# A hybrid attention layer on one core: low weight parts moved to the left end of the buffer, deeper rings for split parts and raw rows, and the order of the last steps' splits

## Chip, cores, metric

One core of a Trainium2 chip. The kernel's time is device microseconds (us) from start to end of one execution; lower is better. A measurement tells two kernels apart when they differ by about 0.5% or more.

## The reference, cut to what matters

One layer over 1024 tokens of width 1024, batch 1, float32:

```python
h = rms_norm(x, mix_norm_g)
u = h @ w_in          # dq, dk, dv | bq, bk, bv | z : 512 columns each, z 1024
dq, dk = rms_norm per 64 columns;  bq, bk = rms_norm per 64 columns
a = diff_attention(dq, dk, dv)     # 4 heads, two softmaxes each, subtracted, ALiBi; then rms_norm
b = dilated_attention(bq, bk, bv)  # 8 heads, windows (128,1) (512,4) (2048,16), merged, ALiBi
y = concat([a, b]) * silu(z)
x = x + y @ w_out
x = x + sigmoid(rms_norm(x, ple_norm_g) @ w_ple_gate) * (p @ w_ple_proj)
```

## The kernel before

Every float32 operand of a large product is split into a high and a low part (hi by a ScalarE copy that rounds, lo = source - hi on VectorE or GpSimd), and a product is three matmuls: hi*hi, hi*lo, lo*hi. The program runs in four stages.

**Stage 1** (0 to 158 us) projects bq, bk and bv from h. It writes bv, bq and bk split to memory outside the core. **Stage 2** (158 to 384 us) runs the eight heads of the dilated attention; the projections of dq, dk and dv are its filler. A step handles one unit (head, kind, u): scores of the unit two ahead (`scores`, L593), their minimum (`least`, L613, VectorE) and exponentials (`exps`, L622, ScalarE), four transposes of this unit (`turn`, L633 and L640 to L645) into one of two PSUM buffers with the tag `t` (pool `ps_t`), the high part by ScalarE (L646), the low part by VectorE (L651, this frees the buffer), and the value products of the unit two back (`values`, L681, L693). Between these `filler(n)` puts n matmuls of the projection (L503, L505, L507). A finished row block of dq or dk (columns c, token tile t) goes by `rows_out` into a `raw` buffer (L426, ScalarE), is squared on GpSimd and summed on VectorE. After four tiles (a group g) a chain of small steps computes factors and scales the four raw blocks (L462, three on GpSimd, one on VectorE). Then the generator `turned(g, ...)` transposes the group in four pieces (L483) into the same two `t` buffers; `cut` splits each piece into `hi` (ScalarE, L469) and `lo` (VectorE, L470, this frees the `t` buffer), and stores both by DMA (L472). `turn_part` advances it by one yield and is called twice in a step: after `turn_lo` and after `values`. The generator first lets TURN_WAIT calls pass. The value blocks of dv go through `v_out` (L417, L418, stores L419) and take their buffers from the same rings, tags `qkhi` and `qklo`.

**Stage 3** (384 to 661 us) runs the differential attention in 36 steps, with the z projection and the first two blocks of the output projection as filler (`z_part(n)`, n matmuls, called a tick each; `pending` holds calls that are due after so many ticks). `weights_at(m, at)` splits weight block m: high part on ScalarE (L895) after `at` ticks, low part on GpSimd (L900) four ticks later. `values(k, 1)` leaves a closure in `slot` that reads the finished PSUM buffer (squares, L1167, on ScalarE; a product into `asb`, L1169, on VectorE); `in_slot` runs it at the start of the next step. The one buffer of that pool also takes `pss` (L1185). `y_split` (L1247, L1248) splits a finished y block. **Stage 4** is the rest of the output projection and the gate.

**Order.** In stage 2 the order on TensorE and GpSimd is the order of the program text; ScalarE, VectorE and the SP queue (nearly all DMAs) are put in order by a planner. In stage 3 all five are in program order, but for the first loads and z products, which the planner places; the loads `td`, `qs`, `kh`, `kl`, `vd` and the first `zraw` carry a raised priority.

**Buffers.** A stage's pools are stacked from the left end or from the right end of each partition. A tile in a place that an earlier tile held waits for that tile's last reader. Bytes within a partition (from the built program):

```
left end                                   right end
stage 1  weights raw    74240 -  90624     (x, later squares 172544-, split rows bq/bk/bv 176640-186880)
         raw rows       90624 - 119296
         high, low     119296 - 172544
stage 2  w2r            74240 -  82432     kn 210944-220160  vn 220160-224768  qn -228864
         w2h            82432 -  98816     w2l 194560-210944   tb1 191488-194560
         free           98816 - 113152     raw2 177152-189440  sq2 -191488   tb2 175616-177152
                                           vc 159232-167424  e 167424-175616
                                           ph, oo 144896-159232  hi, lo 136704-144896
                                           pl, fold, extra 125440-136704  qc, kc 113152-125440
stage 3  zraw, zhi, zlo 74240 -  92672     kl_0 216576-224768  kh_0 208384-216576
         kh_1           92672 - 100864     qs 200192-208384    td 196096-200192
         rb            100864 - 104960     kl_1 187904-196096  ed 167424-187904
         zt, vd        104960 - 121344     phd, pld, sqd 141824-167424
```

Of the kernel before, what the change touches and what calls it, by code (L numbers as in the profile page):

```python
# [8 lines left out]
F32 = mybir.dt.float32  # L9
F32R = mybir.dt.float32r  # L10
# [8 lines left out]
P = 128  # L19
# [23 lines left out]
OUT_AT = 2  # L43
SUM_AT = 12
SPLIT_AT = 6
TURN_WAIT = 5
FOLD_AT = 1
CL_AT = {(1, 3): (0, 1), (0, 0): (2,)}
LAG = 2
# [22 lines left out]
def tile_hybrid_layer(ctx: ExitStack, tc, xT, w_att, w_z, w_o, w_g, w_p, pT, vec, lamv, tdil, tdiff, outT):  # L72
# [67 lines left out]
    def pool(name, bufs=1, **kw):  # L140
        return tc.tile_pool(name=name, bufs=bufs, reuse_waits="tile", **kw)
# [42 lines left out]
    with ExitStack() as pa:  # L184
# [77 lines left out]
        for d in range(8):  # L262
            g = vec_sb[:, C_G1 + d : C_G1 + d + 1]
            b, a = divmod(d, 2)
# [98 lines left out]
    with ExitStack() as pb:  # L363
        wpr = pb.enter_context(pool("w2r"))
        wph = pb.enter_context(pool("w2h"))
        np_ = pb.enter_context(pool("np", side="right"))
        wpl = pb.enter_context(pool("w2l", side="right"))
        tbp = pb.enter_context(pool("tbp", side="right"))
        ap_ = pb.enter_context(pool("ap2", side="right"))
        tbq = pb.enter_context(pool("tbq", side="right"))  # L370
        bpa = pb.enter_context(pool("bpa", side="right"))
        bpb = pb.enter_context(pool("bpb", side="right"))
        aq = pb.enter_context(pool("aq2", side="right"))
        bp = pb.enter_context(pool("bp", side="right"))
        cq = pb.enter_context(pool("cq", side="right"))
        ps_m = pb.enter_context(pool("ps_m", 2, space=PSUM))
        ps_t = pb.enter_context(pool("ps_t2", 2, space=PSUM))
        ps_s = pb.enter_context(pool("ps_s", 2, space=PSUM))
# [5 lines left out]
        turns, turns_done = [], []  # L384
# [11 lines left out]
        def proj():  # L396
# [15 lines left out]
            def v_out(t, ps):  # L412

                for a in range(2):
                    vt = aq.tile([P, 2, 2, P], F32R, tag="qkhi" if a else "qklo", bufs=2, name=f"v2_{t}_{a}")
                    v = ps[:, a * 256 : a * 256 + 256].rearrange("p (h w) -> p h w", w=P)
                    A.activation(vt[:, :, 0, :], v, AF.Copy, scale=rstd[:, t : t + 1])  # L417
                    V.scalar_tensor_tensor(out=vt[:, :, 1, :], in0=v, scalar=rstd[:, t : t + 1], in1=vt[:, :, 0, :].bitcast(F32), op0=ALU.mult, op1=ALU.subtract)  # L418
                    nc.sync.dma_start(dv_d[t * P : (t + 1) * P, 2 * a : 2 * a + 2].rearrange("t h w -> t (h w)"), vt.rearrange("p h a w -> p (h a w)").bitcast(F32))  # L419


            def rows_out(c, t, ps, ss, raws):
                g = 2 * c + t // 4
                assert 4 * g + t % 4 < 6 or divmod(4 * g + t % 4 - 6, 4) in turns_done
                raw = ap_.tile([P, 512], F32, tag="raw", bufs=6, name=f"raw2_{c}_{t}")
                A.copy(raw, ps)  # L426
                sq = ap_.tile([P, 512], F32, tag="sq", bufs=1, name=f"sq2_{c}_{t}")
                G.tensor_mul(sq, raw, raw)
                raws.append((raw, sq))
# [34 lines left out]
            def cut(g, p_, fh, tp):  # L464
                n, t0 = ("dq", "dk")[g // 2], 512 * (g % 2) + 256 * p_
                gain = qk_scale(n)
                tv = tp.rearrange("p f a w -> p f (a w)")
                hi, lo = (aq.tile([P, 2, 256], F32R, tag=f"qk{k}", bufs=2, name=f"{k}2_{g}_{p_}_{fh}") for k in ("hi", "lo"))
                A.activation(hi, tv, AF.Copy, scale=gain)  # L469
                V.scalar_tensor_tensor(out=lo, in0=tv, scalar=gain, in1=hi.bitcast(F32), op0=ALU.mult, op1=ALU.subtract)  # L470
                for s_, tl in enumerate((hi, lo)):
                    nc.sync.dma_start(qk_d[n][2 * fh : 2 * fh + 2, :, s_, t0 : t0 + 256].rearrange("f p t -> p f t"), tl.bitcast(F32))  # L472
# [302 lines left out]
    with ExitStack() as pb:  # L775
# [106 lines left out]
        def zpath():  # L882
# [52 lines left out]
            def weights_at(m, at):  # L935
                pending.append([at, lambda: split_hi(m)])
                pending.append([at + 4, lambda: split_lo(m)])
# [52 lines left out]
            for f in range(2):  # L990
                for half in range(2):
                    held[f, half] = (ps_s[0] if f else ps_z).tile([P, 512], F32, tag="s" if f else "z", name=f"pso_{f}_{half}")
                if f == 0:
                    for h in range(2):
                        weights_at(18 + h, 3 + 23 * h)
                wo[f] = [ws[16 + 2 * f + b] for b in range(2)]
                for ds in (range(4), range(4, 6)):
                    for half in range(2):
                        for d in ds:
                            for _ in out_products(f, half, d):  # L1000
                                yield
# [242 lines left out]
        def y_split(i, half, src):  # L1244
            y_tile(i, half)
            hi, lo = y[half][i]
            A.copy(hi, src)  # L1247
            V.tensor_sub(lo, src, hi.bitcast(F32))  # L1248
# [33 lines left out]
        def in_slot():  # L1282
            for f in slot:
                f()
            slot.clear()

        def step(g):
# [36 lines left out]
            if g - 1 in Y_IN:  # L1324
                y_diff(*Y_IN[g - 1])
            if g in (32, 33):
                y_split(6, g - 32, ga[2, g - 32][0])
            if g == 33:
                bit(100)
# [271 lines left out]
```

## Time and profile before

| | us |
|---|---|
| median of 3 runs | 844.51 (844.06 to 846.97) |
| the profiled execution: its own time | 845.52 |
| its span in the trace | 843.6 |
| TensorE busy / granted clock over the span | 820.1 (97%) / 0.992 |
| VectorE, ScalarE, GpSimd busy | 541.6, 458.0, 335.2 |

Busy time is the sum of the instructions' durations where they don't overlap. The granted clock is the share of full speed that TensorE was given; it has two levels, 2.4 GHz (1.00) and 1.2 GHz (0.50), so a mean between them is a mixture. In a timeline row the brackets hold the engine's idle time just before the instruction and what ended it.

### The profile page before, as it was taken

Reading aid. Unit: us, or ns where it says so; the run is one execution under the profiler, and the core shown is the slowest. Engines: PE = TensorE matmul, PEld = TensorE weight load, DVE = VectorE, ACT = ScalarE, POOL = GpSimd, SP = SyncE. Lnnn points to the kernel's source line nnn. Section 1 sums busy time; section 2 is a strip of 40 time slices with the busy share of each in tenths; the row PEclk is TensorE's granted clock in tenths of the full one; section 3 lists DMA queues with packets and bytes.
Section 4 is the critical chain, followed back from the end, with each engine's and each line's share of the span. In section 5 each row is a group of like instructions: output and inputs, shape, how many; then the busy total and the mean of one; then the engine's idle time right before and its main releaser. Section 6 shows DMA issues by size and latency. Waiting matters only on the chain.

```text
span 843.6 us, 13212 instructions
## 1 busy us (share of the span) xinstructions
PE 820.1 (97%) x4364; PEld 696.3 (83%) x4364; DVE 541.6 (64%) x1264; ACT 458.0 (54%) x940; POOL 335.2 (40%) x391
## 2 busy tenths in 40 slices
PE   9999999999999999998999999999998999999997
PEld 8888888888878888887678878888787888888886
DVE  6948543467867686765688777778774573544432
ACT  8653433466766776664487876787671343321210
POOL 5503020145763555022278888785572243200000
PEclk9999999999999999999999999999999999999999
DMA  7612679558768679838597683944491574524210
GB/s 248 215 62 62 205 211 322 156 119 240 208 183 203 184 213 273 236 103 232 153 230 190 184 254 114 271 126 151 161 388 38 176 261 149 175 102 149 88 50 37
DMA packets 112468, 150.21 MB, mean 178 GB/s; under 512 B 11008, under 2 KB 70032, under 8 KB 112400
## 3 DMA queue, kind: packets, MB, share of 16 engines
q1 hardware_dynamic: 109376, 144.00, 56.7%
q10 hardware_dynamic: 3024, 5.38, 2.0%
q8 instruction: 34, 0.56, 0.3%
q14 instruction: 34, 0.28, 0.1%
HBM read 101.95 MB, written 47.39 MB: 177 GB/s over the span
## 4 chain that ended last, share of the span: by engine, by line
PE 80%; POOL 5%; DMA 4%; DVE 4%; ACT 3%; issue 2%; SPq 1%; DVEq 0%; POOLq 0%; ACTq 0%
PE mm L253 5%; PE mm L255 5%; PE mm L254 5%; PE mm L503 5%; PE mm L507 5%; PE mm L505 5%; PE psg L1401 3%; PE psg L1402 3%; PE psg L1403 3%; PE s L593 3%; PE pso L1403 3%; PE pso L1401 3%; PE pso L1402 3%; POOL ed L1122 2%; PE sd L1098 2%; PE sd L1099 2%
## 5 line engine op out<-in xcount | busy, mean ns | idle before, releaser
L1122 POOL TENSOR_TENSOR ed<-ed,ed 128x512 f32<-128x512 f32 x64 | 82.1, 1304 | 51.1 <-ACT ed L1120 34.1
L1110 ACT ACTIVATE ed<-ed,nm 128x1024 f32<-128x1024 f32 x64 | 73.8, 1153 | 45.9 <-DVE nm L1101 45.9
L622 ACT ACTIVATE e<-e,stats 128x256 f32<-128x256 f32 x128 | 64.7, 508 | 30.8 <-DVE stats L613 30.5
L503 PE MATMUL mm<-w2h,h_hi 128*128 128x512 f32 x192 | 79.0, 412 | 0.7 <-ACT raw L426 0.7
L505 PE MATMUL mm<-w2l,h_hi 128*128 128x512 f32 x192 | 79.5, 414 | 0.0
L507 PE MATMUL mm<-w2h,h_lo 128*128 128x512 f32 x192 | 76.7, 400 | 0.0
L254 PE MATMUL mm<-wl,h_hi 128*128 128x512 f32 x192 | 75.3, 392 | 0.0
L255 PE MATMUL mm<-wh,h_lo 128*128 128x512 f32 x192 | 75.1, 391 | 0.0
L253 PE MATMUL mm<-wh,h_hi 128*128 128x512 f32 x192 | 74.5, 394 | 0.0
L613 DVE CUSTOM_DVE_ANT_0 e<-s,tb 128x256 f32<-128x256 f32 x128 | 48.8, 418 | 18.6 <-PE s L593 18.0
L651 DVE TENSOR_TENSOR pl<-t,ph 128x512 fp32r<-128x512 f32 (+2 forms) x72 | 45.1, 627 | 19.9 <-ACT ph L646 17.7
L1101 DVE CUSTOM_DVE_ANT_0 ed<-sd,td,nm 128x512 f32<-128x512 f32 x64 | 48.1, 751 | 12.3 <-PE sd L1099 3.3
L1098 PE MATMUL sd<-kh,qs 128*128 128x512 f32 x128 | 54.2, 423 | 0.8 <-DVE nm L1101 0.4
L1101 DVE CUSTOM_DVE_ANT_0 ed<-sd,td 128x512 f32<-128x512 f32 x64 | 43.9, 686 | 14.8 <-PE sd L1099 11.7
L943 PE MATMUL psz<-h_hi,zhi 128*128 128x512 f32 x128 | 50.7, 396 | 1.1 <-ACT zhi L895 1.1
L947 PE MATMUL psz<-h_hi,zlo 128*128 128x512 f32 x128 | 50.8, 397 | 0.6 <-POOL zlo L900 0.6
L1099 PE MATMUL sd<-kl,qs 128*128 128x512 f32 x128 | 50.7, 396 | 0.7 <-DMA kl<-dk_d 0.7
L945 PE MATMUL psz<-h_lo,zhi 128*128 128x512 f32 x128 | 50.7, 396 | 0.0
L646 ACT CAST ph<-t 128x512 fp32r<-128x512 f32 (+2 forms) x72 | 38.2, 532 | 22.9 <-PE t L633 13.4
L1143 DVE TENSOR_TENSOR pld<-td,phd 128x512 fp32r<-128x512 f32 x64 | 42.2, 687 | 12.8 <-ACT phd L1134 12.3
L1401 PE MATMUL psg<-h,wh_g 128*128 128x512 f32 x128 | 50.0, 391 | 0.0
L1403 PE MATMUL psg<-h,wl_g 128*128 128x512 f32 x128 | 49.8, 389 | 0.0
(283 smaller groups left out, 2325.5 us busy)
## 6 DMA issues: line engine op xcount, KB each, us to landing
kn<-bk_d SPq DMA_DIRECT2D x16, 512.0 KB, 7.1
w2r<-in_w_att_dram SPq DMA_DIRECT2D x24, 256.0 KB, 4.3
y<-yd_d SPq DMA_DIRECT2D x12, 512.0 KB, 6.8
x<-in_xT_dram SPq DMA_DIRECT2D x16, 256.0 KB, 5.4
wr<-in_w_att_dram SPq DMA_DIRECT2D x8, 512.0 KB, 3.8
qn<-bq_d SPq DMA_DIRECT2D x16, 256.0 KB, 4.1
bv_d<-bv SPq DMA_DIRECT2D x16, 256.0 KB, 4.4
vc<-bv_d SPq DMA_DIRECT2D x32, 128.0 KB, 4.6
```

Of the source, the lines that this page charges most:

```text
L253: T.matmul(ps, h_hi[d][:, ts_], wh, start=(d == 0), stop=False)
L254: T.matmul(ps, h_hi[d][:, ts_], wl, start=False, stop=False)
L255: T.matmul(ps, h_lo[d][:, ts_], wh, start=False, stop=(d == 7))
L503: T.matmul(ps, h_hi[d][:, ts_], wh, start=(d == 0), stop=False)
L505: T.matmul(ps, h_hi[d][:, ts_], wl, start=False, stop=False)
L507: T.matmul(ps, h_lo[d][:, ts_], wh, start=False, stop=(d == 7))
L1098: T.matmul(ps, q, kh[:, c, hs], start=True, stop=False)
L1101: V.tensor_tensor_reduce(out=sp[:, hs], in0=ps, in1=td[:, off : off + 512], scale=4.0 ** -(hd + 1), scalar=BIG if half == 0 else nm[:, 0:1 ...
L1110: A.activation(sp, sp, AF.Exp, bias=nm[:, 1:2], scale=-1.0, accum_out=l)
L1122: G.tensor_add(w[:, hs], w[:, hs], e1[:, hs])
L1401: T.matmul(ps, hi[:, d, :], xh, start=(d == first), stop=False)
L1403: T.matmul(ps, lo[:, d, :], xh, start=False, stop=(d == last))
```

## The change

In stage 2 the pool of the low weight parts (`w2l`) goes from the right end to the left end, behind `w2h`, where stage 1 had its raw rows. The rings of `qkhi` and `qklo` get four buffers each for two, the ring `raw` eight for six, and TURN_WAIT is 8 for 5. The pools `cq` (qc, kc) and `aq2` (hi, lo) change places with `bpb` (ph, oo) and `bp`. In stage 3 the second half of weight block 19 is split after 33 ticks for 26, and in steps 32 and 33 `in_slot` is called ahead of `y_split`.

```diff
-TURN_WAIT = 5
+TURN_WAIT = 8
@@ stage 2, pools
         wpr = pb.enter_context(pool("w2r"))
         wph = pb.enter_context(pool("w2h"))
+        wpl = pb.enter_context(pool("w2l"))
         np_ = pb.enter_context(pool("np", side="right"))
-        wpl = pb.enter_context(pool("w2l", side="right"))
         tbp = pb.enter_context(pool("tbp", side="right"))
         ap_ = pb.enter_context(pool("ap2", side="right"))
         tbq = pb.enter_context(pool("tbq", side="right"))
         bpa = pb.enter_context(pool("bpa", side="right"))
+        cq = pb.enter_context(pool("cq", side="right"))
+        aq = pb.enter_context(pool("aq2", side="right"))
         bpb = pb.enter_context(pool("bpb", side="right"))
-        aq = pb.enter_context(pool("aq2", side="right"))
         bp = pb.enter_context(pool("bp", side="right"))
-        cq = pb.enter_context(pool("cq", side="right"))
@@ v_out
-                    vt = aq.tile([P, 2, 2, P], F32R, tag="qkhi" if a else "qklo", bufs=2, name=f"v2_{t}_{a}")
+                    vt = aq.tile([P, 2, 2, P], F32R, tag="qkhi" if a else "qklo", bufs=4, name=f"v2_{t}_{a}")
@@ rows_out
-                assert 4 * g + t % 4 < 6 or divmod(4 * g + t % 4 - 6, 4) in turns_done
-                raw = ap_.tile([P, 512], F32, tag="raw", bufs=6, name=f"raw2_{c}_{t}")
+                assert 4 * g + t % 4 < 8 or divmod(4 * g + t % 4 - 8, 4) in turns_done
+                raw = ap_.tile([P, 512], F32, tag="raw", bufs=8, name=f"raw2_{c}_{t}")
@@ cut
-                hi, lo = (aq.tile([P, 2, 256], F32R, tag=f"qk{k}", bufs=2, name=f"{k}2_{g}_{p_}_{fh}") for k in ("hi", "lo"))
+                hi, lo = (aq.tile([P, 2, 256], F32R, tag=f"qk{k}", bufs=4, name=f"{k}2_{g}_{p_}_{fh}") for k in ("hi", "lo"))
@@ zpath, first block of the output projection
-                        weights_at(18 + h, 3 + 23 * h)
+                        weights_at(18 + h, 3 + 30 * h)
@@ step of stage 3
             if g in (32, 33):
+                in_slot()
                 y_split(6, g - 32, ga[2, g - 32][0])
```

## Rows read from the trace of the kernel before

**Rows 1.** The page's first part: busy time, share of the span and instructions of each engine.

```profile
PE 820.1 (97%) x4364; PEld 696.3 (83%) x4364; DVE 541.6 (64%) x1264; ACT 458.0 (54%) x940; POOL 335.2 (40%) x391
```

**Rows 2.** TensorE's waits over the whole span: what waited for what; us in total, how often, the longest.

```profile
PE pss L1185 <- DVE asb L1169: 2.1, 1, 2.1
PE tp L483 <- POOL raw L462: 2.0, 2, 1.5
PE tp L483 <- DVE lo L470: 1.6, 1, 1.6
PE t L633 <- DVE lo L470: 1.2, 1, 1.2
...
PE psz L943 <- ACT zhi L895: 1.1, 1, 1.1
...
PE sd L1099 <- DMA kl<-dk_d: 0.7, 1, 0.7
PE mm L503 <- ACT raw L426: 0.7, 1, 0.7
PE psz L947 <- POOL zlo L900: 0.6, 1, 0.6
```

**Rows 3.** Busy time by stretch: the stretch and its length, then busy us (instructions) of TensorE, weight loads, VectorE, ScalarE and GpSimd, then TensorE's granted clock, the DMA engines' share and GB/s.

```profile
210.00:220.00 10.00, 10.00 (x64) 8.68 (x63) 9.54 (x22) 7.81 (x19) 7.11 (x8) 1.00 0.72 211
...
235.00:240.00 5.00, 2.98 (x16) 2.23 (x15) 3.94 (x11) 2.80 (x8) 4.92 (x5) 0.97 0.86 281
240.00:245.00 5.00, 5.00 (x27) 4.45 (x25) 2.79 (x7) 2.49 (x7) 3.48 (x4) 0.69 0.55 158
...
320.00:330.00 10.00, 8.43 (x56) 7.33 (x55) 6.75 (x17) 6.09 (x17) 4.97 (x9) 1.00 1.00 275
...
410.00:415.00 5.00, 5.00 (x17) 3.92 (x16) 3.15 (x7) 3.06 (x7) 2.69 (x3) 0.66 0.29 105
...
600.00:605.00 5.00, 4.38 (x18) 3.75 (x18) 3.46 (x11) 3.60 (x6) 2.41 (x3) 0.66 0.74 254
...
640.00:645.00 5.00, 2.71 (x13) 2.63 (x14) 2.74 (x6) 0.00 (x0) 0.96 (x1) 0.74 0.00 0
```

**Rows 4.** Timeline of TensorE around two of group 0's transposes and one of group 1's, and of GpSimd's scaling of group 1: start, duration, engine, line, operation, count.

```profile
201.87 0.60 PE L483 MATMUL tp<-ident,raw 128*128 128x128 f32 x4
205.32 0.60 PE L483 MATMUL tp<-ident,raw 128*128 128x128 f32 x4
...
238.67 0.55 PE L483 MATMUL tp<-ident,raw 128*128 128x128 f32 x3 [1.54 <-POOL raw L462]
...
235.20 4.42 POOL L462 TENSOR_TENSOR raw<-raw,fac_dq 128x512 f32<-128x512 f32 x3
```

**Rows 5.** Timeline of VectorE, SP and ScalarE around the two late cuts, and, from the view of one line, the time from issue to landing of the four stores of line 419 between 310 and 332 us.

```profile
296.58 0.75 DVE L470 SCALAR_TENSOR_TENSOR lo<-tp,vec_sb,hi 128x512 fp32r<-128x512 f32 x1 [2.43 <-DMA dk_d<-lo]
...
318.49 0.54 SPq L419 DMA_DIRECT2D dv_d<-v  x1
...
327.03 0.69 ACT L469 ACTIVATE hi<-tp,vec_sb 128x512 fp32r<-128x512 f32 x1 [2.37 <-PE o L693]
...
DMA to landing us min/median/max: 5.0/5.7/8.4
```

**Rows 6.** Timeline of TensorE, SP and VectorE at the change from stage 2 to stage 3, and the load of `rb` with its time to landing.

```profile
383.88 0.28 PE L693 MATMUL o<-pl,vn 128*128 128x256 f32 x1
...
383.72 0.33 SPq L790 DMA_DIRECT2D td<-in_tdiff_dram  x1
386.82 2.98 SPq L810 DMA_DIRECT2D kl<-dk_d  x4
402.60 1.06 SPq L890 DMA_DIRECT2D zraw<-in_w_z_dram  x2
...
138.44 0.43 SPq L1338 DMA_DIRECT2D rb<-rs_d  x1
DMA to landing us min/median/max: 7.4/7.4/7.4
...
395.28 0.70 DVE L952 TENSOR_TENSOR psz<-psz,rb 128x512 f32<-128x512 f32 x1 [4.66 <-PE psz L947]
```

**Rows 7.** Timeline of VectorE, ScalarE and GpSimd in the last steps of stage 3.

```profile
638.35 0.16 DVE L110 TENSOR_TENSOR dtmp<-dfac 128x4 f32<-128x4 f32 x1
638.55 1.21 DVE L112 SCALAR_TENSOR_TENSOR dtmp<-dtmp,sub 128x4 f32<-128x4 f32 x1
640.90 0.68 DVE L1248 TENSOR_TENSOR y<-ya,y 128x512 fp32r<-128x512 f32 x1
641.58 0.41 DVE L1169 TENSOR_TENSOR asb<-od,zt 128x256 f32<-128x256 f32 x1
...
637.75 0.62 ACT L895 CAST zhi<-zraw 128x512 fp32r<-128x512 f32 x1 [1.71 <-PE pso L1013]
...
638.45 1.29 POOL L900 TENSOR_TENSOR zlo<-zraw,zhi 128x512 fp32r<-128x512 f32 x1 [2.20 <-ACT zhi L895]
```

**Rows 8.** Timeline of ScalarE and GpSimd where stage 2 takes over from stage 1.

```profile
159.02 1.07 ACT L426 COPY raw<-mm 128x512 f32<-128x512 f32 x2 [4.48 <-DVE stats L613]
...
109.45 2.01 POOL L571 CAST qc<-qn 128x1024 fp32r<-128x1024 f32 x1
159.69 1.04 POOL L428 TENSOR_TENSOR sq<-raw 128x512 f32<-128x512 f32 x1 [47.92 <-ACT raw L426]
```

## The prediction

> **What bounds the kernel now.** I read the page first: TensorE is busy 820.1 of 843.6 us [rows 1], the next engine 541.6. So nothing but TensorE's own time sets the end, and an edit can win only what TensorE loses: idle time, and time at the lower clock. The second view is therefore the list of TensorE's waits [rows 2]. The reader is to see that the waits are few, each with its own cause, and that eight of them lie at places that the diff touches: 2.1 + 2.0 + 1.6 + 1.2 + 1.1 + 0.7 + 0.7 + 0.6 = 10.0 us. The third view, busy time by stretch [rows 3], shows what a wait costs behind it. After the idle time in 235 to 240 the granted clock is 0.69 in the next 5 us: between the levels of 1.00 and 0.50 that is (1 - 0.69) x 5 = 1.55 us of lost work, and 0.15 in the stretch before, together 1.7. In 410 to 415 it is 0.34 x 5 = 1.7, in 640 to 645 0.26 x 5 = 1.3. Not every wait brings it: after the 1.6 us in 320 to 330 the clock is 1.00, yet it fell to 0.66 in 600 to 605, where TensorE idled for only 0.6. I take the clock's loss where the rows show it, and give no rule for it. The fourth view is the timeline at each wait, for its cause.
>
> **The change part by part.** Which tile lies over which follows from the sizes in the table of buffers. After the change, from the left: w2l 98816-115200. From the right: tb1 207872-210944, raw and sq 189440-207872, tb2 -189440, vc 171520-179712, e -187904, kc and qc 159232-171520, hi and lo 142848-159232, oo and ph 128512-142848, then pl, fold, extra from 117248.
>
> *First raw copies.* raw2 lies over stage 1's split rows of bv, and its first copy waits until 159.02 [rows 8], though ScalarE was idle for 4.48 us. The last stores of bv are what it waits for, in my reading of the addresses. Afterwards it lies over tiles of x, long free. TensorE's wait of 0.7 for it [rows 2] goes: **-0.7**. In exchange e comes over the split rows; e is first written at about the time of that copy, so I put it at nothing (at worst the same 0.7 comes back). The copy into qc, 2.01 us, has to wait for stage 1's last weights, because qc now lies over them; GpSimd stands idle for 47.92 us up to 159.69 [rows 8], which hides it. w2l over the raw rows costs nothing: w2h, which is written first, lay over raw rows that are freed no earlier.
>
> *TURN_WAIT 8.* Three more calls at two in a step are 1.5 steps. Two transposes of a group, one step apart, start at 201.87 and 205.32 [rows 4], so a step is 3.45 us and a group's transposes move 5.2 us later. In group 1 the scaling on GpSimd ends at 235.20 + 4.42 = 239.62, and the transposes wait for it, the last of them until 238.67 [rows 4], 2.0 us in all [rows 2]; 5.2 us later nothing is left of that. With the clock behind it: 2.0 + 1.7 = **-3.7**. The eight raw buffers are what lets the transposes come later; they cost nothing by themselves.
>
> *Four buffers for hi and lo.* At 296.58 a cut on VectorE waits 2.43 us for the store of an older `lo` [rows 5], and a transpose of the attention behind it waits 1.2 for the `t` buffer [rows 2]. At 327.03 ScalarE's `hi` has idled 2.37 us; the row names TensorE, but the ring gives this `hi` the buffer of the dv block whose store was issued at 318.49, and one of those stores took 8.4 us [rows 5]: 318.5 + 8.4 = 326.9. The next transpose waits 1.6 for its `lo`. Two buffers more and both stores are two turns older: **-1.2 and -1.6**. No clock was lost behind either (1.00 in 320 to 330), and none is won.
>
> *w2l on the left.* Stage 3's td, qs and kh lie over w2l, kn and tb1 before, so td is issued at 383.72, after the last product with w2l, and the SP queue then works off td, qs, kh, kl (the last four from 386.82), stores and more loads until it gets to `zraw` at 402.60 [rows 6]. From this come the waits for kl (0.7), for the z block's high part (1.1) and its low part (0.6), and the clock of 410 to 415. Afterwards td and qs lie over raw rows and tb1, kh over tb1 and kn, and all of these are freed while head 7 still has steps to go. kl still lies over vn, read until 383.88 + 0.28 [rows 6], so it gains only 386.82 - 384.2 = 2.6 us at issue, but it has the five loads from td to kh no longer right ahead of it. `zraw` moves up by what the loads issued earlier no longer take, by my estimate 5 to 10 of the 18.9 us between 383.72 and 402.60. I take all of it: 0.7 + 1.1 + 0.6 + 1.7 = **-4.1**; the other end is nothing, if the planner's order of the queue is no better. In exchange `rb` and the first vd come over w2l. rb was loaded at 138.44, is first used at 395.28, and took 7.4 us [rows 6]: from 384 it lands at 391, with 4 us to spare, cost nothing if it is issued before 387.9; what it costs behind that is a rival below.
>
> *The last steps.* `pss` waits 2.1 us for L1169 at 641.58 [rows 2, 7], since both use one PSUM buffer. With `in_slot` first, L1169 goes ahead of the L1248 of `y_split`, which starts at 640.90: it wins 641.58 - 640.90 = 0.7. The 33 ticks put block 19's high part behind that closure on ScalarE, so that it can't hold the squares back; but it waited for TensorE until 637.75 [rows 7] and still would. What holds L1169 further is L112, in front of it in either order: 1.21 us beside GpSimd's L900, where its like takes 0.16 [rows 7]. L900 follows the high part, so it stays at about 638.45. So 0.7 of the 2.1; and, since the wait left (1.4) is shorter than 1.6, which cost no clock, also the 1.3: **-2.0**, with 0.7 and 3.4 as bounds.
>
> The Trainium skill, "SBUF — State Buffer", section "SBUF: two separate sides", says that a VectorE operation with two SBUF inputs and a GpSimd operation that reads SBUF exclude one another: whichever comes second is blocked until the first is through. The row of L112 agrees (1.21 for 0.16). It speaks against this part of the change: by it L1169 gains only the 0.7, and without it the sum would have the whole 2.1.
>
> *New waits.* The moved cuts, a ScalarE and a VectorE instruction each, 0.69 and 0.75 [rows 5], meet other work: group 0's last two come into 210 to 220, where VectorE is busy 9.54 of 10 [rows 3]. Nothing shows what that does. Bounds: nothing, and all 16 cuts late at 1.2 to 1.6 each. I take one late cut and one fall of the clock, 1.3 + 1.7 = **+3.0**, since of the 16 cuts only the two named caused a wait before.
>
> Sum: -0.7 - 3.7 - 1.2 - 1.6 - 4.1 - 2.0 + 3.0 = -10.3. The profiled execution took 845.52, its span and 1.9 around it, and stands 1.0 above the median of the runs. 845.5 - 10.3 = 835.2, and as a median 844.5 - 10.3 = **834.2**.
>
> **The rivals.**
> *The queue wins nothing at the change of stage.* The planner may put rb behind kl and the stores, where `zraw` is now: issued at 399 it lands at 406, VectorE's L952 comes 11 us late, and everything behind it on VectorE, the first scores too. For it: rb has no raised priority. Against: rb is free to go before kl is. The 4.1 are lost and some 2 more: 834.2 + 6 = 840. Chance 0.17.
> *Everything goes well.* No new waits, and L112 slips in ahead of L900, so that all of the 2.1 and 1.3 is won: 834.2 - 3.0 - 1.4 = 829.8, rather less if a wait not counted goes too. Chance 0.12.
> *The waits only move.* VectorE, ScalarE and GpSimd carry 40 to 64% on average [rows 1], so a wait removed may come back a step later. For it: VectorE's 9.54 of 10; against: the stretches of idle time have causes of their own. 843 to 846. Chance 0.13.
> *Slower: cuts late as a rule.* The `t` buffers are two, shared by attention and cuts. If the moved cuts come too late for the next user of their buffer, each stops TensorE for 1.2 to 1.6. The gain of 13.3 is eaten from ten late cuts of 16 on, or from five, if each brings a fall of the clock; all 16 without the clock give 844.5 - 13.3 + 22.4 = 853.6. For it: 9.54 in 210 to 220. Against: a cut has a whole step of 3.45 us for 1.44 us of work. Chance 0.05.
> That the change doesn't do what it says would show as td still at 383.7; it is part of the first rival.
>
> **How the numbers follow.** My forecast, 830.5 to 838, has 0.53. With the first rival and the low one the range is 828 to 842; outside lie half of "the waits only move", the slow case and a little below. No measurement of this kernel tells less than 0.5%, 4.2 us, from no change. Faster than 840.3: 0.53 + 0.12 + two thirds of 0.17 and a little of the next = 0.77. Within: 0.17. Slower: 0.06.
>
> **What would show it.** Right: td issued before 370; no wait of L483 for L462, and none of L483 or L633 for L470; the `zraw` loads that stood at 402.60 before 398; 1.00 in the stretches that answer to 240 to 245 and 410 to 415; pss waiting 1.4 for L1169, which starts ahead of L1248, and the row of L112 still near 1.2. Wrong: an SP row of rb behind the stores and L952 waiting for it; new waits of L633 for L470 in 205 to 220 or 300 to 310; TensorE's busy time falling little while its waits stay at some 10 us under other names.

## The result and the profile after

The kernel after takes 837.26 us, the median of five runs (835.42 to 839.28), against 844.51 (844.06 to 846.97) before: a ratio of 0.9906, interval 0.9884 to 0.9929. Run again, it took 835.50 (833.97 to 839.40) against 844.55 for the kernel before beside it, a ratio of 0.9899 (0.9873 to 0.9924). So it is faster by 0.9 to 1.0%. The forecast was 834.2, the range 828 to 842.

The profiled execution of the kernel after took 839.28 us of its own time, 837.5 of span; it was the slowest of the five. First its page's busy times and TensorE's waits, as in [rows 1, 2]:

```profile
PE 814.2 (97%) x4364; PEld 690.8 (82%) x4364; DVE 547.5 (65%) x1264; ACT 457.8 (55%) x940; POOL 334.2 (40%) x391
...
PE sd L1099 <- DMA kl<-dk_d: 2.8, 1, 2.8
...
PE tp L483 <- DVE lo L470: 2.1, 2, 1.0
PE t L643 <- DVE pl L651: 1.7, 2, 1.5
...
PE pss L1185 <- DVE asb L1169: 1.4, 1, 1.4
...
PE sd L1098 <- DMA kl<-dk_d: 0.7, 1, 0.7
PE s L593 <- DVE stats L613: 0.4, 1, 0.4
```

The reader is to see that of the eight waits in [rows 2] three names are left: `pss` at 1.4 instead of 2.1, `tp` for L470, which has another cause now (below), and kl, at 0.7 + 2.8 instead of 0.7. Beside them stand waits that were not there or were small: L651 1.7, L613 0.4, and `sd` for L1101 1.2 instead of 0.4. TensorE's idle time, summed over its timeline, is 18.65 us before and 18.67 after. By this pair of profiles the change won no idle time at all; what it won is the clock. The stretches, to be held against [rows 3]:

```profile
235.00:240.00 5.00, 5.00 (x33) 4.37 (x32) 4.63 (x14) 3.35 (x9) 5.00 (x6) 1.00 0.79 242
240.00:245.00 5.00, 5.00 (x35) 4.47 (x34) 3.35 (x9) 3.65 (x11) 3.41 (x5) 1.00 0.24 53
395.00:400.00 5.00, 5.00 (x16) 3.94 (x17) 3.55 (x8) 1.73 (x3) 0.00 (x0) 0.66 0.91 287
600.00:605.00 5.00, 4.20 (x23) 3.27 (x22) 2.80 (x8) 2.27 (x5) 4.25 (x8) 1.00 0.18 70
635.00:640.00 5.00, 3.37 (x23) 2.74 (x22) 3.65 (x7) 0.00 (x0) 1.89 (x2) 1.00 0.00 0
```

Before, four falls cost 1.7 us each, some 6.8 in all; here there is one, 0.34 x 5 = 1.7 at 395, and another behind TensorE's last product, where it costs nothing. That is 5.1 of the 6.1 us between the spans. Of the falls that are gone, the one at 601 is not the change's to win: it stands behind waits of 0.3 and 0.6 us that all the profiles have, and it comes again in e4 (0.69 in 600 to 605) and in e11 (0.69 in 590 to 595), which has all the edits of the change, with a turn of 7. Nor is it worth its whole 1.7: in these three profiles the next wait of `sd` for L1101, 0.8 us in the eleven others, is missing. And a single pair misleads, as the second profile of the same kernel shows: a span of 832.7, 14.75 us idle, and no fall of the clock while TensorE works. Against the profile of before that is 3.9 us of idle time and 6.8 of clock. So the experiments are read by stretch, and a wait counts as the kernel's own only where it stands in several profiles.

### The profile page after: what moved, and what is told of

Read it like the earlier page. It is cut to its first block, busy times and chain, and to the rows that moved or that the text cites. A ratio compares the mean times of both kernels' runs of the same rounds, so it can differ in the third digit from the quotient of the medians.

```text
span 837.5 us, 13211 instructions
## 1 busy us (share of the span) xinstructions
PE 814.2 (97%) x4364; PEld 690.8 (82%) x4364; DVE 547.5 (65%) x1264; ACT 457.8 (55%) x940; POOL 334.2 (40%) x391
## 4 chain that ended last, share of the span: by engine, by line
PE 79%; DVE 7%; POOL 4%; DMA 3%; issue 3%; ACT 3%; SPq 0%; DVEq 0%; POOLq 0%; ACTq 0%
PE mm L253 5%; PE mm L255 5%; PE mm L254 5%; PE mm L503 4%; PE mm L507 4%; PE mm L505 4%; PE psg L1402 3%; PE psg L1404 3%; PE psg L1403 3%; PE s L593 3%; PE pso L1403 3%; PE pso L1402 3%; PE pso L1404 3%; POOL ed L1122 2%; PE sd L1098 2%
## 5 line engine op out<-in xcount | busy, mean ns | idle before, releaser
L507 PE MATMUL mm<-w2h,h_lo 128*128 128x512 f32 x192 | 75.8, 395 | 0.0
L253 PE MATMUL mm<-wh,h_hi 128*128 128x512 f32 x192 | 74.1, 392 | 0.0
L613 DVE CUSTOM_DVE_ANT_0 e<-s,tb 128x256 f32<-128x256 f32 x128 | 48.8, 418 | 21.9 <-PE s L593 16.4
L1101 DVE CUSTOM_DVE_ANT_0 ed<-sd,td 128x512 f32<-128x512 f32 x64 | 43.9, 686 | 22.0 <-PE sd L1099 18.7
L651 DVE TENSOR_TENSOR pl<-t,ph 128x512 fp32r<-128x512 f32 (+2 forms) x72 | 45.2, 628 | 18.6 <-ACT ph L646 16.5
L1101 DVE CUSTOM_DVE_ANT_0 ed<-sd,td,nm 128x512 f32<-128x512 f32 x64 | 48.1, 751 | 12.7 <-PE sd L1099 3.8
L1402 PE MATMUL psg<-h,wh_g 128*128 128x512 f32 x128 | 50.0, 391 | 0.0
L1403 PE MATMUL psg<-h,wh_g 128*128 128x512 f32 x128 | 49.8, 389 | 0.0
```

The lines of the kernel that those rows point to most:

```text
L253: T.matmul(ps, h_hi[d][:, ts_], wh, start=(d == 0), stop=False)
L507: T.matmul(ps, h_lo[d][:, ts_], wh, start=False, stop=(d == 7))
L1101: V.tensor_tensor_reduce(out=sp[:, hs], in0=ps, in1=td[:, off : off + 512], scale=4.0 ** -(hd + 1), scalar=BIG if half == 0 else nm[:, 0:1 ...
L1402: T.matmul(ps, hi[:, d, :], xh, start=(d == first), stop=False)
L1403: T.matmul(ps, hi[:, d, :], xl, start=False, stop=False)
```

## Experiments

One table first. The three last columns come from the timeline of TensorE in each profile: from the end of stage 1 (last L253) to the end of stage 2 (last L507); from there to the first transpose of stage 3 (L1133), which is the change of stage; from there to the last `pss`.

| kernel | median us | ratio to before (95%) | stage 2 | change of stage | stage 3 |
|---|---|---|---|---|---|
| before | 844.51 | | 231.6 | 33.3 | 237.3 |
| after | 837.26 | 0.9906 (0.9884 to 0.9929) | 228.7 | 33.5 | 234.6 |
| e9: after, again | 835.50 | 0.9899 (0.9873 to 0.9924) | 226.8 | 29.4 | 234.8 |
| e2: pools alone | 837.83 | 0.9915 (0.9889 to 0.9940) | 232.1 | 29.4 | 236.3 |
| e3: rings and turn | 841.70 | 0.9955 (0.9938 to 0.9973) | 226.1 | 35.7 | 237.7 |
| e4: last steps alone | 843.76 | 0.9973 (0.9955 to 0.9991) | 230.8 | 32.3 | 238.6 |
| e5: TURN_WAIT 8, 8 raw | 841.31 | 0.9933 (0.9908 to 0.9959) | 226.1 | 34.2 | 238.5 |
| e6: four buffers alone | 842.55 | 0.9963 (0.9942 to 0.9984) | 227.8 | 35.9 | 239.1 |
| e1: after, rb behind kl | 834.57 | 0.9865 (0.9844 to 0.9887) | 226.7 | 27.8 | 235.8 |
| e7: e1, TURN_WAIT 6 | 832.14 | 0.9831 (0.9804 to 0.9858) | 225.0 | 27.8 | 235.6 |
| e8: e1, in_slot early | 832.72 | 0.9838 (0.9811 to 0.9866) | 226.8 | 27.8 | 235.3 |
| e10: e1, TURN_WAIT 6, in_slot early | 831.32 | 0.9852 (0.9827 to 0.9877) | 225.3 | 27.8 | 233.7 |
| e11: e1, TURN_WAIT 7 | 832.88 | 0.9863 (0.9839 to 0.9887) | 227.2 | 27.8 | 235.7 |
| e12: e1, two buffers | 835.25 | 0.9890 (0.9862 to 0.9918) | 228.7 | 27.8 | 236.3 |

e1 to e4 share their runs of before (median 845.95), e5 to e8 theirs (845.92), e9 to e12 theirs (844.55). The three groups ran on three chips, so kernels of different groups are compared by their ratios.

### The change of stage: rb at the head of the queue (e1, e9, e2)

In the profile of after the SP queue and TensorE's two waits read so, against [rows 6]:

```profile
364.59 0.42 SPq L790 DMA_DIRECT2D td<-in_tdiff_dram  x1
372.86 2.12 SPq L419 DMA_DIRECT2D dv_d<-v  x2
380.18 0.32 SPq L1339 DMA_DIRECT2D rb<-rs_d  x1
380.59 1.23 SPq L804 DMA_DIRECT2D kh<-dk_d  x2
381.91 4.28 SPq L810 DMA_DIRECT2D kl<-dk_d  x4
395.71 2.24 SPq L890 DMA_DIRECT2D zraw<-in_w_z_dram  x3
...
391.55 0.47 PE L1098 MATMUL sd<-kh,qs 128*128 128x512 f32 x1 [0.66 <-DMA kl<-dk_d]
394.85 0.48 PE L1099 MATMUL sd<-kl,qs 128*128 128x512 f32 x1 [2.83 <-DMA kl<-dk_d]
```

`td` goes out 19 us earlier than before, as forecast. Then the queue stands still from 375 to 380.18: `rb`, which now lies over w2l, is next, and kh waits behind it.

e1, the kernel after with

```diff
-                nc.sync.dma_start(t[64 * a : 64 * a + 64].bitcast(F32), qk_d["dk"][hd, 64 * c : 64 * c + 64, 1, :])
+                ks["load"] = nc.sync.dma_start(t[64 * a : 64 * a + 64].bitcast(F32), qk_d["dk"][hd, 64 * c : 64 * c + 64, 1, :])
...
-        nc.sync.dma_start(rb, rs_d.rearrange("(o a) b -> o (a b)", o=1).broadcast_to([P, S]))
+        with tc.issue_after(ks["load"].ins): nc.sync.dma_start(rb, rs_d.rearrange("(o a) b -> o (a b)", o=1).broadcast_to([P, S]))
```

> The kernel after, with one edit: the load of rb is issued after the last load of the first kl, where the kernel after has it ahead of kh. Theory (the queue is held up by its head): in the kernel after, rb waits for the last product with w2l until 380.18 us, and kh, whose place is free by about 366, stands behind it in the same queue; so kh and kl land together, TensorE waits 0.7 + 2.8 us for kl, and the clock then falls once (1.7 us). With rb behind kl, kh is issued before 374, kl still not before 380.2 (its place holds vn until then), TensorE's wait for kl is under 1.0 us, the granted clock in the stretch behind it is 1.00, and the time is 837.3 - 3 to 5 = 832 to 834 us. Rival 1 (kl's own place decides): kl is issued no earlier than 380 and lands as late as before, the wait of 2.8 us stays: 836 to 838. Rival 2 (rb becomes the late one): VectorE's L952 waits for rb by 2 us or more, and the scores behind it come late: 836 to 840.

```profile
373.15 1.23 SPq L804 DMA_DIRECT2D kh<-dk_d  x2
378.72 2.38 SPq L810 DMA_DIRECT2D kl<-dk_d  x4
383.39 0.58 SPq L1339 DMA_DIRECT2D rb<-rs_d  x1
```

Against the end of stage 2 (378.46 here, 380.38 in after) kh goes out 5.5 us earlier than in after, kl 1.3; no wait of sd for a load is left, no fall of the clock, and the change of stage takes 27.8 us. It took 27.8 in all six profiles that have this edit. The time, 834.57, is 0.6 above the expected range, which started from 837.3; the ratio, 0.9865, makes 833.1 of the 844.51 there and lies inside it. No L952 waits for rb, as the second rival had it. The theory holds: one load that waits for its place cost what stood behind it in the queue.

How much it costs in the kernel after, e9 tells, the same kernel once more:

> The kernel after, unchanged, beside the three others of this call. Theory (rb ahead of kh is the cause and stands in every execution; the wait of L643 for L651 is not): the stretch from the last L507 to the first L1133 is 33.4 us again, within 0.6, with waits of sd for kl of 3 to 4 us and one fall of the clock behind them; the wait of L643 for L651 near 305 us, 1.5 before, is under 0.5 or at another place, and the stretch from the last L253 to the last L507 is 226.7 to 227.5 us instead of 228.7; 836.5 to 839.5 us, a ratio of 0.989 to 0.992. Rival (the queue's order was right and the profiled execution was a bad one): the first stretch is 29 to 31 us.

```profile
379.23 0.32 SPq L1339 DMA_DIRECT2D rb<-rs_d  x1
379.64 1.23 SPq L804 DMA_DIRECT2D kh<-dk_d  x2
380.96 3.36 SPq L810 DMA_DIRECT2D kl<-dk_d  x4
...
390.93 0.47 PE L1099 MATMUL sd<-kl,qs 128*128 128x512 f32 x1 [0.75 <-DMA kl<-dk_d]
392.89 0.47 PE L1099 MATMUL sd<-kl,qs 128*128 128x512 f32 x1 [0.33 <-DMA kl<-dk_d]
```

rb is ahead of kh here too, but kl lands in time for all but 1.1 us, and the clock does not fall: 29.4 us, so of the two theories the rival won on the size, and the time, 835.50, is below the range expected. The queue's order costs 29.4 - 27.8 = 1.6 in this execution and 33.5 - 27.8 = 5.7 in the first (waits 3.5, clock 1.7, the rest 0.5). Why the same loads took longer there (a median of 11.8 us from issue to landing for kl, 8.9 in e9, 4.4 in e1) is open. By the ratios, 0.9906 and 0.9899 against 0.9865, rb costs some 3 us; this is an estimate, for the intervals still touch.

e2, the kernel before with the pools alone in their new order:

```diff
+            wpl = pb.enter_context(pool("w2l"))
             np_ = pb.enter_context(pool("np", side="right"))
-            wpl = pb.enter_context(pool("w2l", side="right"))
...
+            cq = pb.enter_context(pool("cq", side="right"))
+            aq = pb.enter_context(pool("aq2", side="right"))
             bpb = pb.enter_context(pool("bpb", side="right"))
```

> The kernel before with the new order of the pools alone (w2l at the left end, cq and aq2 in their new places); rings of two, six raw rows, TURN_WAIT 5 and the last steps as before. Theory: the pools by themselves are worth the 0.7 us of the first raw copies and, at the change of stage, next to nothing, since a load that lies over w2l (here the first vd) stands ahead of kh in the queue: td is issued before 370 us, but kl not before 380, and the first td product of the third stage is no earlier against the end of the second stage than before; 842.5 to 844.5 us, a ratio of 0.998 to 1.000. Rival (the prediction's step): the 4.1 us of the change of stage are won here: 839 to 841, a ratio of 0.994 to 0.996.

```profile
379.14 0.37 SPq L814 DMA_DIRECT2D vd<-dv_d  x1
379.61 1.23 SPq L804 DMA_DIRECT2D kh<-dk_d  x2
384.69 2.39 SPq L810 DMA_DIRECT2D kl<-dk_d  x4
```

My theory fell: the pools alone win at the change of stage, 33.3 to 29.4, although a fall of the clock (1.7) is in the 29.4 as it is in the 33.3. So the 3.9 are the waits of 0.7, 1.1 and 0.6 and some 1.4 more that no row names, and none of it is clock. A load that lies over w2l does stand ahead of kh, but it is vd, issued right behind the stores at 379.14, 5 us ahead of the end of stage 2 at 384.4: its place was free. rb has gone behind kl by itself. So w2l on the left can be worth the 4.1 us, and more (e1); it was the planner's choice of rb or vd, which came out differently with other rings, that spoilt it. The median is lower still, by 0.85% or 7.2 us, than even the rival had it, where the three stretches of the profiled execution, one of the two slowest of six, are shorter by 4.4. What wins the rest isn't shown.

### Stage 2: two edits that take away the same wait (e3, e5, e6, e12)

e3 is the kernel before with TURN_WAIT 8, eight raw rows and four buffers; e5 has the first two of these alone, e6 the four buffers alone. The first diff is in e3 and e5, the second in e3 and e6, `v_out` likewise:

```diff
-TURN_WAIT = 5
+TURN_WAIT = 8
...
-                raw = ap_.tile([P, 512], F32, tag="raw", bufs=6, name=f"raw2_{c}_{t}")
+                raw = ap_.tile([P, 512], F32, tag="raw", bufs=8, name=f"raw2_{c}_{t}")
```

```diff
-                hi, lo = (aq.tile([P, 2, 256], F32R, tag=f"qk{k}", bufs=2, name=f"{k}2_{g}_{p_}_{fh}") for k in ("hi", "lo"))
+                hi, lo = (aq.tile([P, 2, 256], F32R, tag=f"qk{k}", bufs=4, name=f"{k}2_{g}_{p_}_{fh}") for k in ("hi", "lo"))
```

> The kernel before with the rings and the turn alone: four buffers for high and low parts, eight raw rows, TURN_WAIT 8; pools and last steps as before. Theory: the end of the second stage comes 2.5 to 3.5 us earlier, by the clock that no longer falls behind the wait of L483 for L462 (1.7), that wait itself (2.0) and the two waits behind stores (2.8), less the new waits of L483 for L470 and of L643 for L651 (some 3.8), and nothing of it is lost later: 840.5 to 842.5 us, a ratio of 0.996 to 0.998. Rival (the new waits come from the pools' move, not from the later turn): no wait of L483 for L470 above 0.5 us here, and the stage is 6 to 7 us shorter: 837 to 839.

> The kernel before with TURN_WAIT 8 and the eight raw rows that it needs, and nothing else (rings of two, pools and last steps as before). Theory (the prediction's step of 3.7 us is right, and the late cuts belong to it): no wait of L483 for L462 (2.0 before), no fall of the clock in 235 to 245, and two new waits of L483 for L470 of about 1.0 each, near 211 and 295 us; the waits for stores (1.2 and 1.6) stay. From the last product of the first stage to the last L507, 231.6 us before, 229 to 231; 841.5 to 844 us, a ratio of 0.995 to 0.998. Rival (the new waits come from the larger rings): no wait of L483 for L470 near 211 and 295; 227 to 228.5 us, a ratio of 0.993 to 0.995.

> The kernel before with four buffers for high and low parts and nothing else. Theory (the prediction's step of 2.8 us is right): the waits of L483 for L470 (1.6) and of L633 for L470 (1.2) are gone, those of L483 for L462 (2.0) and the clock's fall behind them stay; 228.5 to 229.5 us from the last product of the first stage to the last L507 against 231.6, and a ratio of 0.995 to 0.998. Rival (the store was not what held the cut; the row names TensorE): the waits stay, and the stage is within 0.8 us of before, 0.999 to 1.001.

TensorE's waits between 160 and 378 us, all that the view has of e5, and then of e6:

```profile
PE tp L483 <- DVE lo L470: 2.1, 2, 1.1
PE t L643 <- DVE pl L651: 0.2, 1, 0.2
PE t L633 <- DVE pl L651: 0.2, 1, 0.2
```

```profile
PE tp L483 <- POOL raw L462: 2.0, 2, 1.6
```

e6 confirms the step of 2.8: both waits behind stores are gone, the wait for L462 and the clock behind it stay (0.82 and 0.84 in 235 to 245), and the stage is 3.8 shorter (2.1 to 3.1 were expected). 3.1 of this are waits that the rows name; the rest, which e1, e3 and e5 have too, I can't assign. e5 refutes both its theory and its rival: the later turn alone takes away the wait for L462 and the clock, as forecast, and both waits behind stores as well, so that the stage falls by 5.4 and not by the 0.6 to 2.6 expected; and the new waits are there with rings of two. They stand in e3 as well (1.05 and 1.04), with the old pools, so that e3's rival is out too, and its stage is shorter by 5.4 where 2.5 to 3.5 were expected. With the turn at 8 the four buffers add nothing: 226.1 with two (e5), 226.1 with four (e3). For the wait near 328 the mechanism is the one that the prediction gave for the four buffers: a cut that comes 5.2 us later finds the store of 318.5 + 8.4 [rows 5] landed. In e5 the store of that dv block goes out 13.5 us ahead of the cut, against 8.5 before:

```profile
311.87 1.02 SPq L419 DMA_DIRECT2D dv_d<-v  x2
325.41 0.68 ACT L469 ACTIVATE hi<-tp,vec_sb 128x512 fp32r<-128x512 f32 x1
```

The wait near 297 went another way, since there the store is that of a cut two earlier and moves along: before, it stood in the queue behind loads of vn and kn, from its cut at 285.78 to 289.41; in e5 it goes out at 287.92, 0.8 us behind the start of its cut.

"Nothing of it is lost later" fell with e3: the change of stage takes 35.7 us there, 34.2 in e5 and 35.9 in e6, against 33.3. The view of the waits has the z block's high part (L895) late by 2.7, 1.5 and 2.6 us instead of 1.1 [rows 2]. In e3 and e5 the waits make up the difference; in e6 those of [rows 2] come to 2.6 in all against 2.5, and what is longer is the time at the lower clock: 0.86 on average over the stretch against 0.95 before, 5 us lost instead of 1.7. In e3 the `zraw` loads go out at 398.57, 4.0 us earlier than in [rows 6], where stage 2 ends 6.5 earlier. Without the new pools, the queue behind w2l gives back a part of what stage 2 wins in e3 and e5. So the parts don't add up: alone they give 0.85 + 0.45 + 0.27 = 1.6%, together 0.9 to 1.0.

e12 asks the same in the kernel after (with rb behind kl), `bufs=4` back to `bufs=2`:

> The kernel of the run with rb behind kl, with two buffers for high and low parts in place of four (eight raw rows and TURN_WAIT 8 as in the kernel after). Theory (the later turn alone already gives the stores their time, as the runs on before with TURN_WAIT 8, with two and with four buffers, had 226.1 us each): no wait of L483 or L633 for an L470 that waits for a store, 226.2 to 227.2 us from the last L253 to the last L507 against 226.7 with four, and a ratio of 0.985 to 0.988. Rival (the four buffers carry their 2.8 us here): waits of 1.2 and 1.6 near 300 and 330 us, 228.5 us or more.

No wait behind a store came back; the two waits for L470 are the same. That the stage took 228.7, within the rival's number, is due to a wait of 1.5 us for L651 that the profile of after has as well, and e1 and e9, with four buffers too, have not. It is not the buffers'. The ratio, 0.9890, lies above the theory's 0.988, though its interval reaches down to 0.9862; that the two buffers cost nothing is shown for the waits, not for the time. The wait for L651 comes about so:

```profile
298.48 5.97 DVE L137 TENSOR_TENSOR w2l<-w2r,w2h 128x512 fp32r<-128x512 f32 x1
304.37 0.68 DVE L651 TENSOR_TENSOR pl<-t,ph 128x512 fp32r<-128x512 f32 x1
...
298.37 1.28 POOL L137 TENSOR_TENSOR w2l<-w2r,w2h 128x512 fp32r<-128x512 f32 x1
299.61 2.04 POOL L571 CAST qc<-qn 128x1024 fp32r<-128x1024 f32 x1
301.62 1.03 POOL L428 TENSOR_TENSOR sq<-raw 128x512 f32<-128x512 f32 x1
302.62 1.28 POOL L137 TENSOR_TENSOR w2l<-w2r,w2h 128x512 fp32r<-128x512 f32 x1
```

This is VectorE and GpSimd of the kernel after. In e1 the same L137 of VectorE starts at 298.52, takes 0.68, and GpSimd's starts behind it at 298.94. Where GpSimd comes first, here by 0.11 us (in e12 by 0.11 as well), VectorE's operation stands until 304.4, through four operations of GpSimd, `pl` is late and TensorE waits. The Trainium skill, "SBUF — State Buffer", section "SBUF: two separate sides", has the rule (a VectorE operation with two SBUF inputs and a GpSimd operation that reads SBUF exclude one another, the first has the port for its whole length); the rows agree, and show beyond it that the one that waits may see several of the other's operations go ahead.

### The new waits: where the later cuts meet VectorE (e7, e11)

In the kernel after the first of the two waits of L483 for L470 comes about so:

```profile
207.95 0.67 ACT L469 ACTIVATE hi<-tp,qgain 128x512 fp32r<-128x512 f32 x1
...
206.31 1.89 DVE L574 CAST kc<-kn 128x1024 fp32r<-128x1024 f32 x1
...
209.29 0.70 DVE L137 TENSOR_TENSOR w2l<-w2r,w2h 128x512 fp32r<-128x512 f32 x1
...
210.57 0.76 DVE L470 SCALAR_TENSOR_TENSOR lo<-tp,qgain,hi 128x512 fp32r<-128x512 f32 x1
...
211.48 0.63 PE L483 MATMUL tp<-ident,raw 128*128 128x128 f32 x4 [1.04 <-DVE lo L470]
```

The high part is ready at 208.6, but the cut stands on VectorE behind the copy into kc, a split of the next weights and, in the rows left out, other work without a gap, and the transposes need its buffer. e7 and e11 are e1 with `TURN_WAIT = 6` and `7`:

> The kernel of the run with rb behind kl, with TURN_WAIT 6 in place of 8, so that a group's transposes and cuts come one step of 3.45 us earlier. Theory (the two waits of L483 for L470, 2.1 us, come from where the cuts meet VectorE's other work, a copy into kc and the splits of the next weights): both are gone or under 0.6 us in all, and the wait for L462, whose scaling ends by the time that the later turn gives, stays away or is under 0.6 us; a ratio to before of 0.983 to 0.986. Rival (less turn brings the wait for L462 back): L483 waits for L462 by 1 us or more, and the clock falls near 240 us: 0.987 to 0.991.

> The kernel of the run with rb behind kl, with TURN_WAIT 7. Theory (what decides is what else VectorE has to do when a cut comes, so the stage's time jumps with the phase of the turn rather than falling or rising with its length): at 7 the waits of L483 for L470 and L462 together are between 0 and 2.5 us, and the stretch from the last L253 to the last L507 lies between the 225.0 of 6 and the 226.7 of 8; a ratio of 0.982 to 0.988. Rival (a longer turn always costs more): the same, but by half the difference, 225.7 to 226.1.

TensorE's waits for L470 between 160 and 376 us, in e7 and then in e11:

```profile
PE tp L483 <- DVE lo L470: 0.9, 1, 0.9
```

```profile
PE tp L483 <- DVE lo L470: 2.2, 3, 1.4
```

At 6 one wait of 0.9 is left of the two, and none for L462: the stage falls from 226.7 to 225.0, which 225.3 in e10 repeats. That is short of "under 0.6", but the direction is the theory's. At 7 there are three waits for L470, 2.2 us in all, and 227.2: more than at 6 and at 8, outside the bounds that I gave. By these three lengths, what the turn changes is which of VectorE's operations the cuts fall upon; it is no dial.

### The last steps (e4, e8, e10)

e4 is the kernel before with the two edits of the last steps:

```diff
-                        weights_at(18 + h, 3 + 23 * h)
+                        weights_at(18 + h, 3 + 30 * h)
...
             if g in (32, 33):
+                in_slot()
                 y_split(6, g - 32, ga[2, g - 32][0])
```

> The kernel before with the edits of the last steps alone (block 19's split seven ticks later, in_slot ahead of y_split in steps 32 and 33). Theory: pss waits 1.4 us instead of 2.1, and the clock no longer falls in 640 to 650, which cost 1.75 us: 842 to 843 us, a ratio of 0.997 to 0.998, and no difference from the kernel before ahead of 600 us. Rival (the clock's fall only moves to a later stretch): 843.8 to 844.5, a ratio of 0.999 to 1.000.

`pss` waits 1.4, as in every profile with these two edits and not that of e8; the time falls by 0.27% or 2.3 us, near the 2.0 that the step said. But the profiled execution, the second slowest of its twelve, does not show it: its stage 3 is 1.3 us longer than before, and the clock fell behind that wait all the same (0.79 and 0.87 in 640 to 650). On average the clock does give something back: from span and granted clock of each timed execution, (1 - clock) x span, it took 3.6 us in the twelve of e4 and 4.9 in the 21 of before, 1.4 less with a standard error of 0.6. With the 0.7 of the wait that is about the 2.3. Of VectorE and GpSimd in the kernel after:

```profile
634.53 1.17 DVE L112 SCALAR_TENSOR_TENSOR dtmp<-dtmp,sub 128x4 f32<-128x4 f32 x1
635.73 1.19 DVE L114 SCALAR_TENSOR_TENSOR dfac<-dtmp,dfac 128x4 f32<-128x4 f32 x1
636.84 0.41 DVE L1169 TENSOR_TENSOR asb<-od,zt 128x256 f32<-128x256 f32 x1
...
634.39 1.28 POOL L900 TENSOR_TENSOR zlo<-zraw,zhi 128x512 fp32r<-128x512 f32 x1 [2.17 <-ACT zhi L895]
635.63 1.26 POOL L1331 TENSOR_TENSOR asb<-asb,zt 128x512 f32<-128x512 f32 x1
```

L112 and L114, of 16 bytes a partition, end within 0.05 us of L900 and L1331 each time, and L1169 comes behind them. e8 is e1 with one more edit in step 32, which puts L1169 ahead of the pair:

```diff
-                values(k - 2, 1)
+                values(k - 2, 1); g == 32 and in_slot()
```

> The kernel of the run with rb behind kl, with one more edit: in step 32 the closure of in_slot is issued right behind the products that it reads, which puts L1169 ahead of a pair L112 and L114 on VectorE; these took 1.20 and 1.19 us there, beside L900 and L1331 of GpSimd, where their likes take 0.16. Theory (what keeps pss waiting is this pair in front of L1169): the pair is as slow as before, but L1169 starts 2.0 us earlier, the wait of pss for L1169 (1.4) is gone, and the stretch from the first L1133 to the last pss is 1.4 us shorter; 833 to 834 us, a ratio 0.001 to 0.003 below that of the run with rb alone. Rival (pss then waits for something else as long, the products in front of it or the sqd of ScalarE): pss starts no earlier against the first L1133, and the ratio is the same within 0.001.

```profile
628.19 0.42 DVE L1169 TENSOR_TENSOR asb<-od,zt 128x256 f32<-128x256 f32 x1
628.52 0.98 DVE L112 SCALAR_TENSOR_TENSOR dtmp<-dtmp,sub 128x4 f32<-128x4 f32 x1
629.54 1.19 DVE L114 SCALAR_TENSOR_TENSOR dfac<-dtmp,dfac 128x4 f32<-128x4 f32 x1
631.32 0.15 DVE L1186 COPY ssq<-pss 128x2 f32<-128x2 f32 x1
...
631.52 0.39 PE L1157 MATMUL od<-phd,vd 128*128 128x256 f32 x1 [1.46 <-DVE ssq L1186]
```

The pair did hold `pss`: its wait is gone. But the pair now stands ahead of L1186, which empties the buffer for the next `od`, and that waits 1.46 instead of 0.25. 1.38 won, 1.21 given back: the same buffer, one user later. The stretch is 0.5 us shorter, not 1.4; the ratio is 0.0027 below that of e1, and the two intervals overlap.

e10 puts the three edits together:

> The three edits together: rb behind kl, in_slot early in step 32, TURN_WAIT 6. Theory (they lie in different stages and add up): 225.0 us from the last L253 to the last L507, 27.8 from there to the first L1133, and pss without a wait; 831 to 833 us, a ratio of 0.981 to 0.984. Rival (the wait of 1.5 that od now has for ssq takes the whole of the last edit): the same, with a ratio not below that of the run with TURN_WAIT 6 (0.983).

It keeps each stage's gain (225.3, 27.8, no wait of `pss`) and has the lowest median, 831.32, 0.5% under the 835.50 of the kernel after, run beside it. The ratio, 0.9852, is above the 0.981 to 0.984 expected and above e7's 0.9831, each within the other's interval: what in_slot adds to the turn isn't shown by the time.

## Why the prediction was right, and where not

What the prediction named to look for came out so: `td` at 364.59, before 370; no wait of L483 for L462; `zraw` at 395.71, before 398; 1.00 in 235 to 245; `pss` at 1.4 with L1169 ahead of L1248. Against it: the waits for L470, and a fall of the clock at the change of stage after all.

*First raw copies, -0.7.* The wait for L426 is gone, but 0.4 of it came back as the wait for L613, which writes e. This row stands in every profile with the new pools and in none without: the "nothing" for e coming over the split rows was the wrong end of its bounds. That the copy waited for a store of bv, read from addresses, is borne out by e6, where its row at 158.54 reads `[4.34 <-DMA bv_d<-bv]`. And in e3 and e5, with eight raw rows and the later turn but the old pools, the first copy runs at 153 and neither wait is there: this term could be had without the new pools and without the 0.4.

*TURN_WAIT, -3.7.* Right, wait and clock both: in e5 neither is there, and e6, without the later turn, has them.

*Four buffers, -2.8.* The waits went, and in e6 by these buffers. In the kernel after the later turn alone would have done it (e5 and e3, e12). The prediction took the two edits one by one, each against the kernel before, and did not ask what the first left for the second; the sum does not suffer, since each wait is in it once, but the 2.8 stand under an edit that was not needed. That part of the hit is luck.

*w2l on the left, -4.1.* Right in mechanism where rb isn't in the way, and near in size: 3.9 in e2, where the clock's 1.7 was not won and 1.4 without a name were, and 5.5 with rb behind kl (33.3 to 27.8), with both. The step that failed is the one on rb: "from 384 it lands at 391, with 4 us to spare, cost nothing if it is issued before 387.9". It asked when rb is needed, not what stands behind it. It was issued at 380.18, well within the limit, and cost kh and kl their head start; in the profiled execution the whole term was lost (33.5), in the second 0.2 of it (29.4). With rb out of the way the kernel is at 0.9865 x 844.51 = 833.1 (e1), and the forecast was 834.2; that the two are so near is in part luck, since the terms beside it are off in both directions. The rival "the queue wins nothing" had the place right and the order wrong: rb ahead of kh, not behind kl.

*Last steps, -2.0.* 1.38 us of waiting, as worked out, with L112 at 1.17. The 1.3 of the clock leaves out 645 to 650, where it was 0.91: with that the fall cost 1.7, and it is won only in some executions. Behind a wait of 1.4 it fell in e4, e7, e11 and e12, and not in after, e9 and e1; behind 2.1 in before, e3, e5 and e6, and not in e2. That a wait below 1.6 costs no clock was read from one row, and is refuted.

*New waits, +3.0.* The size was about right, the make-up not: two late cuts of 1.0 instead of one of 1.3, no fall of the clock behind them, and 0.5 (e9) or 1.9 (after) for L651.

*The clock in the sum.* Its net share in the sum was 1.7 + 1.7 + 1.3 - 1.7 = 3.0 us. From span and granted clock of each timed execution, (1 - clock) x span, the mean is 4.9 over 49 executions of before and 2.6 over 11 of after: 2.3 won. Both means count falls behind TensorE's last product, which cost nothing: 1.0 of the 2.7 us in the profile of after, none in that of before, so that 2.3 may be too low. By this estimate a quarter to a third of the 7.3 to 9.1 us is clock, or somewhat more, where the first pair of profiles says clock alone.

Of the rivals, "the waits only move" fits the profiled pair (18.65 and 18.67 idle), not the second profile; "cuts late as a rule" is out, with 2 of 16.

## What to carry to other kernels

A load that must wait for its place stops its whole queue: when tiles are moved, look for each load at what it now lies over and at what stands behind it in the queue, not only at when its own data is needed. Two edits that shift the same ring in time are to be priced together, since one may leave nothing for the other. And where waits of some 1.5 us and falls of the clock come and go between executions of one kernel, read a second profile before naming where a gain of 1% went.

## What was not expected of the hardware

In stage 2, which of two operations came first by 0.1 us decided over 5.3 us on VectorE (L137, 5.97 or 0.68 us) and 1.5 us on TensorE. The clock fell behind waits of 1.4 us in four of seven profiles, and behind no wait but 1.1 + 0.3, which all fourteen profiles have, in two (0.69 in 390 to 395 in e2, 0.66 in 385 to 390 in e6); in the same kernel it may fall or not. Among the 49 executions of before, which spread from 840.9 to 850.0, the time lost to the clock and the time go together with a correlation of 0.57, so that the clock accounts for about a third of the variance and most of it has another cause.
